# Neighbourhood attention in blocks of 16 rows by 8 columns, with q, k and v ordered by grid column

## The chip, the cores and the metric

The kernel runs on one core of a Trainium2 chip. The metric is device time in microseconds of one execution, as the median of several runs; smaller is better. One execution is also profiled, and all views quoted here are of such a profile.

## What is computed

One mixer layer over 1024 tokens of width 1024, in float32. The tokens form a grid of 16 rows by 64 columns (row = t // 64, column = t % 64).

```
h = x @ W_in                          # q, k, v, z of two groups of 8 heads of 64
group A: each token attends to a window of 8 rows x 16 columns of the grid,
         clamped inside it, with a learned bias per head and relative position
group B: each token attends to |i - j| <= 128, rotary q and k, 2 k/v heads, a sink logit
y = concat(A * silu(z_a), B * silu(z_b)) @ W_out
x = LayerNorm(2**0.25 * x + y) * gain + bias
```

The window of group A is `r0 = clip(r - 4, 0, 8)` to `r0 + 8` in rows and `c0 = clip(c - 8, 0, 48)` to `c0 + 16` in columns.

## The kernel before

Every matmul with float32 data is made of 16-bit halves (high and low part): three matmuls for one product. The projections are 21 groups of 128 columns of W_in in the order of the list `ORDER`; 24 matmuls of 512 tokens make one half of a group in a PSUM bank `ps_pj` (line 379). q and k of a head pair are evicted by `split_q` and `split_k`: ScalarE writes the high part (L257), VectorE the low part (L263), and for k GpSimd copies both to the other 64 partitions (`dup_`, L295). Each works on one half of the tokens and one head, a tile of 64 partitions by 512.

Attention goes in 128 units of 128 queries, first the 64 of group B, then the 64 of group A. A unit passes through stages, one step of a loop apart, and each step of the loop issues by hand, for different units, in this order:

- `stage_load` (seven steps ahead): the bias of group A from DRAM (SP queue) and its scaling on GpSimd (L788)
- `stage_qk`: two matmuls (L816, L817) into one of four PSUM banks `ps_s`, then VectorE adds the bias and takes the row's extreme (L826)
- `stage_exp`: the exponential on ScalarE (L842)
- `stage_tr`: the probabilities' high part on ScalarE (L852) and low part on VectorE (L853), and a DMA transpose of both (SP queue)
- `stage_pv`, for four units at once: three matmuls of 64 columns for each chunk of keys (L881); `stage_on` divides by the sum (L890)
- `stage_ot`: four transposes on TensorE (L901), then the product with the gate z on VectorE (L904 for group B, L910 for group A)

Between these, the matmuls of the later projections (`FILL`) and of the first part of the output projection are issued in proportion to the steps: item n of `FILL` starts at step `FILL_AT[n]` and ends at `FILL_AT[n + 1]`. So q0 runs from step 49 to 57, q1 from 66 to 74, q2 from 81 to 89, z2 to 97, k3 to 105, q3 to 112 and z3 to 121. The first unit of group A is at step 64, and each pair of heads (`p`) takes 16 steps. Engines execute their own instructions in the order in which they were issued. `need` issues what a unit depends on if that is still queued, and `pop` issues queued side work, a little per step.

In group A a unit is 8 rows by 16 columns of queries: four column blocks `b`, two halves of the rows. Its keys are 11 or 12 rows of 24 or 32 columns (`NROW`, `WINW`), read from the k tile as rows of a strided view; the softmax and the values take 12 rows, in three chunks of 96 or 128 keys. The q columns are put in the order of blocks by the projection's moving operand. The values are written to DRAM (`vd`, `v_part`), copied there into four column windows (`vwin`, `window`), and loaded from these for each head pair and block (`va`, `gather_v`). The bias is loaded in three pieces for each head.

The tiles `va` (values, and the rotary's scratch) are six buffers of 2 KB a partition, the tiles `bs` (bias) five.

Of the kernel before, what the change touches and what calls it, by code (L numbers as in the profile page):

```python
# [40 lines left out]
WIN_AT = [186, 202, 218, 234]  # L41
VA_AT = [46, 49, 52, 55]
VA_STEP = [(0, 1, 1), (0, 1, 3), (1, 0, 1), (1, 0, 3)]
# [8 lines left out]
WIN0 = (0, 8, 24, 40)  # L52
WINW = (24, 32, 32, 24)
NROW = (11, 12)
NKEY = tuple(12 * w for w in WINW)
BOFF = (0, 23 * WINW[0], 23 * WINW[0], 23 * (WINW[0] + WINW[1]))
BTOT = 23 * (WINW[0] + WINW[1] + WINW[3])
# [4 lines left out]
def hybrid_block(ctx, tc, xT, x, wt, wv, wo, bias, sink, gain, lbias, cos, sin, bmask, out):  # L62
# [15 lines left out]
    vd = dram.tile([4, S, 256], F16, name="vd")  # L78
    vwin = [dram.tile([4, ROWS, WINW[b] * 256], F16, name=f"vwin{b}") for b in range(4)]
# [188 lines left out]

    def split_q(p, half, src, dep=None):
        sl = slice(512 * half, 512 * half + 512)  # L270
# [12 lines left out]
    def split_k(p, half, src, dep=None):  # L283
        sl = slice(512 * half, 512 * half + 512)
# [3 lines left out]
        for j in range(2):  # L288
            a, o = slice(64 * j, 64 * j + 64), slice(64 - 64 * j, 128 - 64 * j)
            hi, lo = split_hl(lambda j=j, a=a: own("kh", p, j)[a, sl], lambda j=j, a=a: own("kl", p, j)[a, sl],  # L290
                              src[a], dep is None, eng)

            def dup_(w, j=j, a=a, o=o):
                t = own(w, p, j)
                nc.gpsimd.tensor_copy(t[o, sl], t[a, sl])  # L295
# [9 lines left out]
    def rope(ps, half):  # L305
# [3 lines left out]
        raw = tiles["ap"].tile([128, 512], F32, tag="va", name="rp_raw", bufs=6)  # L309
        sw = tiles["ap"].tile([128, 512], F32, tag="va", name="rp_sw", bufs=6)  # L310
# [94 lines left out]
    with ExitStack() as vctx:  # L405
# [276 lines left out]
        def v_part(t):  # L682
            if t > 0:
# [52 lines left out]
    def gather_v(p, b):  # L736
        w = WINW[b]
        t = ap.tile([128, 4, 256], F16, tag="va", name=f"va{p}_{b}", bufs=6)
        bulk["last"] = bulk["step"]
        nc.sync.dma_start(t[:4 * w], vwin[b][p].rearrange("(g i) (c e) -> (i c) g e", g=4, e=256))  # L740
        va[p, b] = t

    def unit_list():
        us = []
        for p in range(4):
            for j in range(2):
                for i in range(8):
                    us.append(("b", p, j, i, i % 2 == 1))
        for p in range(4):
            for j in range(2):  # L750
                for b in range(4):
                    for half in range(2):
                        us.append(("a", p, j, (b, half), half == 1))
        return us
# [11 lines left out]
    def geom(u):  # L766
        g, p, j, t, _ = u
        if g == "a":
            b, half = t
            w = WINW[b]  # L770
            return NKEY[b], [4 * w] * 3
        lo, hi = max(t - 1, 0), min(t + 2, 8)
        return 128 * (hi - lo), [128] * (hi - lo)

    def stage_load(u, i):
        g, p, j, t, _ = u
        n, _c = geom(u)
        if g == "a":
            b, half = t
            if half == 0 and b != 2:  # L780
                bulk["last"] = clock["step"] + 1
                bt = ap.tile([128, 23 * WINW[1]], F32, tag="bs", name="bias", bufs=BR)
                o, m = BOFF[b], 23 * WINW[b]
                nc.sync.dma_start(bt[:, :m], bias[2 * p + j, :, o:o + m])
                bv = bt[:, :m]
                ld = Op("sp", None, [], 1)
                ld.step = i
                op = enq("pool", lambda: nc.gpsimd.tensor_scalar(bv, bv, rsg, -1.0, op0=ALU.mult, op1=ALU.mult),  # L788
                         ld, prio=0)
                st["bias"] = bt, op  # L790
            o = 11 * WINW[b] * half
            st[u, "b"] = st["bias"][0][:, o:o + NROW[half] * WINW[b]], st["bias"][1]

    def stage_qk(u):
        g, p, j, t, _ = u
        n, _c = geom(u)
        ps = bank("s")
        m, end = n, 384
        if g == "a":
            b, half = t  # L800
# [4 lines left out]
            bias_t, op = st.pop((u, "b"))  # L805
            need(op)
            init = 3e38
        else:
            q = stks["q", f"b{p}", j][:, 128 * t:128 * t + 128]
            lo = max(t - 1, 0) * 128  # L810
# [5 lines left out]
        nc.tensor.matmul(ps[:, :m], q, sl[0], start=True, stop=False)  # L816
        nc.tensor.matmul(ps[:, :m], q, sl[1], start=False, stop=True)  # L817
        s0 = sns[units.index(u) % 2]
        sn = s0[:, end - m:]
        if g == "b" and t < 2:  # L820
            nc.vector.tensor_copy(s0[:, 384:385], nsk[:, h:h + 1])
        elif units.index(u) == 64:
            nc.vector.memset(s0[:, 384 - WINW[1]:384], -NEG)
        nm = ap.tile([128, 1], F32, tag="nm", name="nm", bufs=6)
        c = min(p, 1) if g == "b" else 2
        nc.vector.tensor_tensor_reduce(sn[:, :m], ps[:, :m], bias_t, sg[:, c:c + 1], init,  # L826
# [18 lines left out]
    def stage_tr(u):  # L845
        g, p, j, t, _ = u
        n, ch = geom(u)
        pt = st.pop((u, "p"))
        c, m = ch[0], len(ch)
        hl = split[units.index(u) % NSPLIT]  # L850
        src = pt[:, :n].rearrange("p (k c) -> p k c", c=c)
        nc.scalar.activation(hl[:, :m, 0, :c], src, AF.Copy, scale=PSCALE)  # L852
        nc.vector.scalar_tensor_tensor(hl[:, :m, 1, :c], src, PSCALE, hl[:, :m, 0, :c],  # L853
# [5 lines left out]
    def quad(q):  # L859
        g, p, j, t, _ = units[4 * q]  # L860
        return g, p, j, t // 4 if g == "b" else t[0] // 2

    def stage_pv(q):
        ps = st[q, "o"] = bank("t")
        for m in range(4):
            u = units[4 * q + m]
            g, p, j, t, _ = u
            n, ch = geom(u)
            tr = st.pop((u, "tr"))
            c = ch[0]  # L870
            mms = []
            for i in range(len(ch)):
                if g == "a":
                    b, half = t
                    v = [va[p, b][:c, i + half, 128 * j + 64 * e:128 * j + 64 * e + 64] for e in range(2)]
                else:
                    v = [vb[:, max(t - 1, 0) + i, p // 2, e, :] for e in range(2)]
                ph, pl = tr[:c, 2 * i, :], tr[:c, 2 * i + 1, :]
# [14 lines left out]
    def stage_ot(q):  # L893
# [11 lines left out]
        else:  # L905
            for i in range(2):
                b = 2 * h + i
                z = zt[p].rearrange("p (r c) -> p r c", c=GW)[:, :, 16 * b:16 * b + 16]
                src = ps[:, 256 * i:256 * i + 256].rearrange("p (r c) -> p r c", c=16)
                nc.vector.scalar_tensor_tensor(z, src, z_col(p), z, op0=ALU.mult, op1=ALU.mult)  # L910

    for b in range(4):
        at(WIN_AT[b], window, b)
# [267 lines left out]
    for i in range(-LD, NU + LO):  # L1181
# [7 lines left out]
        if i in VA_AT:  # L1189
            gather_v(0, VA_AT.index(i))  # L1190
# [22 lines left out]
        if i < NU:  # L1213
            u = units[i]
            if u[3] in (0, 4):
                need(*stk_ops[f"b{u[1]}", u[2], u[3] // 4])
            if u[3] == (0, 0):
# [17 lines left out]
        if 0 <= q < NU // 4:  # L1235
            g, p, j, h = quad(q)
            if g == "a" and p < 3 and (j, h, m) in VA_STEP:
                gather_v(p + 1, VA_STEP.index((j, h, m)))
# [15 lines left out]
def _host(inputs):  # L1254
# [22 lines left out]
    bt = np.full((8, 128, BTOT), NEG, np.float32)  # L1277
    rr, cc = np.divmod(np.arange(128), 16)
    for half in range(2):
        for b in (0, 1, 3):  # L1280
            r, c = rr + 8 * half, cc + 16 * b
            kr = np.repeat(np.arange(NROW[half]) + 4 * half, WINW[b])
            kc = np.tile(np.arange(WINW[b]) + WIN0[b], NROW[half])
            r0, c0 = np.clip(r - 4, 0, 8), np.clip(c - 8, 0, 48)
            ok = ((kr[None] >= r0[:, None]) & (kr[None] < r0[:, None] + 8)
                  & (kc[None] >= c0[:, None]) & (kc[None] < c0[:, None] + 16))
            pi, ki = np.nonzero(ok)
            o = BOFF[b] + half * 11 * WINW[b]
            bt[:, pi, o + ki] = rpb[:, kr[ki] - r[pi] + 7, kc[ki] - c[pi] + 15]
# [35 lines left out]
```

## Time and profile before

| | before |
|---|---|
| median of 3 runs | 447.23 us (445.42 to 447.49) |
| span of the profiled execution | 444.7 us; the time of that execution itself is not listed apart |
| TensorE busy | 437.5 us, 3289 matmuls |
| VectorE, ScalarE, GpSimd busy | 344.2, 308.3, 221.6 us |
| DMA | 81.39 MB in 133841 packets |

The span runs from the first instruction to the last. L12 stands for line 12 of the kernel. PE is TensorE's matmul, PEld its weight loads, DVE VectorE, ACT ScalarE, POOL GpSimd, SP the engine that issues the DMAs. In a row of the timeline stand start and duration in us, the engine, the line, the operation and its tiles; in a row of a group the count, the total busy us, the mean ns of one, and the idle time of the engine just before them with what ended it. In a row of waits stand who waited for whom, and then the total us, the number of waits and the longest.

### The profile page before, as it was taken

The page shows a single profiled execution, that of the slowest core. Times are in us where ns is not written, and L with a number is a line of the kernel's source. Part 1 is how long each engine was busy: PE and PEld are TensorE (multiplying, and loading weights), DVE is VectorE, ACT ScalarE, POOL GpSimd, SP SyncE. Part 2 cuts the span into 40 slices and gives each one's busy share as a digit, 9 for nine tenths or more (in the row PEclk, how much of TensorE's full clock was granted, in tenths as well). Part 3 has the DMA queues.
Part 4 walks back from the last instruction along what each step waited for, and adds up shares of the span by engine and source line. Part 5 has one row for each costly group of instructions (what it writes and reads, how often), then busy time and mean ns, then how long its engine had stood idle before and what let it go on. Part 6 is the DMA issues. An engine that isn't in the chain of part 4 may idle for free.

```text
span 444.7 us, 9505 instructions
## 1 busy us (share of the span) xinstructions
PE 437.5 (98%) x3289; PEld 255.5 (57%) x3289; DVE 344.2 (77%) x849; ACT 308.3 (69%) x700; POOL 221.6 (50%) x235
## 2 busy tenths in 40 slices
PE   9999999999999999999999999999999999999994
PEld 8997754444445565655565655656555654444453
DVE  5978967438986898887988888888878837589944
ACT  5759789766499988887868887888778946302401
POOL 0110074646839558866506767765574405205740
PEclk9999999999999999999999999999999999999997
DMA  8921469984659999587978899998999998103612
GB/s 272 390 91 60 145 235 339 336 292 169 213 127 214 206 190 181 98 162 143 164 127 175 169 182 180 213 170 213 192 204 253 167 172 347 55 0 102 232 69 72
DMA packets 133841, 81.39 MB, mean 183 GB/s; under 512 B 101280, under 2 KB 113440, under 8 KB 133536
## 3 DMA queue, kind: packets, MB, share of 16 engines
q1 hardware_dynamic: 133648, 80.64, 75.4%
q8 instruction: 26, 0.43, 0.4%
q14 instruction: 23, 0.19, 0.2%
q10 hardware_dynamic: 144, 0.13, 0.1%
HBM read 50.34 MB, written 9.96 MB: 136 GB/s over the span
## 4 chain that ended last, share of the span: by engine, by line
PE 91%; DMA 3%; POOL 3%; DVE 1%; issue 1%; ACT 1%; SPq 0%; POOLq 0%; DVEq 0%; ACTq 0%
PE ps_pj L379 44%; PE ps_s L1031 9%; PE ps_s L486 6%; PE ps_t L881 6%; PE ps_pj L1031 5%; PE ps_t L1031 5%; PE ps_s L816 4%; PE ps_s L817 4%; PE ps_pj L486 3%; PE ps_t L486 3%; DMA bias<-in_bias 3%; PE ps_t L901 1%; POOL wl L205 1%; PE ps_t L412 1%; POOL ks L295 1%
## 5 line engine op out<-in xcount | busy, mean ns | idle before, releaser
L379 PE MATMUL ps_pj<-xf,wh 128*128 128x512 f16 x672 | 202.1, 379 | 0.1
L379 PE MATMUL ps_pj<-xf,wl 128*128 128x512 f16 x336 | 127.3, 379 | 0.0
L379 PEld LDWEIGHTS <-wh 128*128 128x128 f16 x672 | 63.7, 98 | 60.4 <-DVE ks L263 0.5
L842 ACT ACTIVATE ps_s<-sn,nm 128x385 f32<-128x385 f32 (+3 forms) x128 | 70.1, 548 | 25.1 <-DVE nm L826 24.6
L853 DVE SCALAR_TENSOR_TENSOR split<-ps_s,split 128x384 f16<-128x384 f32 (+2 forms) x128 | 65.7, 513 | 27.5 <-ACT split L852 25.9
L1031 PEld LDWEIGHTS <-m 128*128 128x128 f16 x432 | 40.0, 98 | 41.1 <-DVE m L939 0.2
L852 ACT ACTIVATE split<-ps_s 128x384 f16<-128x384 f32 (+2 forms) x128 | 57.8, 452 | 2.5 <-DMA tr<-split 0.2
L204 POOL TENSOR_SCALAR wr<-wr,wsc 128x512 f32<-128x512 f32 x26 | 20.6, 791 | 68.1 <-ACT wh L199 61.6
L379 PEld LDWEIGHTS <-wl 128*128 128x128 f16 x336 | 32.9, 98 | 37.4
L826 DVE CUSTOM_DVE_ANT_0 sn<-ps_s,bm,nsk 128x384 f32<-128x384 f32 (+1 forms) x64 | 40.7, 636 | 2.0 <-PE ps_s L817 1.7
L1031 PE MATMUL ps_s<-wo,m 128*128 128x512 f16 (+1 forms) x192 | 40.8, 366 | 0.0
L816 PE MATMUL ps_s<-ks,qs 128*128 128x384 f16 (+4 forms) x128 | 39.2, 306 | 0.3 <-DVE qs L263 0.3
L817 PE MATMUL ps_s<-ks,qs 128*128 128x384 f16 (+4 forms) x128 | 39.2, 306 | 0.0
L826 DVE CUSTOM_DVE_ANT_0 sn<-ps_s,bias,sg 128x264 f32<-128x264 f32 (+1 forms) x64 | 35.0, 547 | 4.5 <-issue 1.5
L881 PEld LDWEIGHTS <-tr 128*128 128x128 f16 (+1 forms) x1104 | 36.6, 98 | 2.2
L205 POOL TENSOR_TENSOR wl<-wr,wh 128x512 f16<-128x512 f32 x26 | 32.7, 1257 | 2.2
L788 POOL TENSOR_SCALAR bias<-bias,rsg 128x552 f32<-128x552 f32 (+1 forms) x24 | 19.1, 797 | 23.8 <-DMA bias<-in_bias 22.6
L295 POOL COPY ks<-ks 64x512 f16<-64x512 f16 x40 | 26.0, 661 | 7.1 <-DVE ks L263 2.8
L1086 ACT ACTIVATE sd<-mv,eps 128x1 f32<-128x1 f32 x8 | 2.4, 295 | 36.5 <-DVE mv L1084 35.2
L1031 PE MATMUL ps_pj<-wo,m 128*128 128x512 f16 (+1 forms) x144 | 26.2, 326 | 0.0
L1130 POOL TENSOR_TENSOR xr<-xr,gb 128x512 f32<-128x512 f32 x7 | 9.8, 1396 | 32.4 <-ACT xr L1127 32.4
L842 ACT ACTIVATION_READ_ACCUMULATOR ps_s<-sn,nm 128x1 f32 x128 | 24.4, 190 | 0.0
(188 smaller groups left out, 813.8 us busy)
## 6 DMA issues: line engine op xcount, KB each, us to landing
ws<-in_wt SPq DMA_DIRECT2D x15, 512.0 KB, 5.9
wr<-in_wt SPq DMA_DIRECT2D x26, 256.0 KB, 3.6
wor<-in_wo SPq DMA_DIRECT2D x22, 256.0 KB, 3.5
bias<-in_bias SPq DMA_DIRECT2D x16, 276.0 KB, 3.3
xr<-in_x SPq DMA_DIRECT2D x8, 512.0 KB, 9.6
out<-xr SPq DMA_DIRECT2D x15, 256.0 KB, 2.1
bias<-in_bias SPq DMA_DIRECT2D x8, 368.0 KB, 3.8
wvraw<-in_wv SPq DMA_DIRECT2D x9, 320.0 KB, 5.8
```

The costliest lines, as they stand in the source:

```text
L205: nc.gpsimd.tensor_sub(l, raw, h)
L295: nc.gpsimd.tensor_copy(t[o, sl], t[a, sl])
L379: nc.tensor.matmul(ps, a[:, k % 4, :], mv, start=(k == 0 and i == 0), stop=(k == KT - 1 and i == 2))
L486: nc.tensor.matmul(ps[:, :320], lh[:, ts], rh[:, cs], start=(k == ko[0] and i == 0), stop=(k == ko[-1] and i == 2))
L816: nc.tensor.matmul(ps[:, :m], q, sl[0], start=True, stop=False)
L817: nc.tensor.matmul(ps[:, :m], q, sl[1], start=False, stop=True)
L826: nc.vector.tensor_tensor_reduce(sn[:, :m], ps[:, :m], bias_t, sg[:, c:c + 1], init, op0=ALU.add, op1=ALU.min, accum_out=nm)
L842: nc.scalar.activation(pt[:, :m], sn[:, :m], AF.Exp, bias=nm, scale=-1.0, accum_out=sm[:, k:k + 1])
L852: nc.scalar.activation(hl[:, :m, 0, :c], src, AF.Copy, scale=PSCALE)
L853: nc.vector.scalar_tensor_tensor(hl[:, :m, 1, :c], src, PSCALE, hl[:, :m, 0, :c], op0=ALU.mult, op1=ALU.subtract)
L881: nc.tensor.matmul(ps[:, HD * m:HD * m + HD], a, b_, start=(i == 0), stop=(i == len(mms) - 1))
L1031: nc.tensor.matmul(ps, lh[:, ts], rh[:, cs], start=(e == EO[0] and i == 0), stop=(e == EO[-1] and i == 2))
```

## The change

A unit of group A is now 16 rows by 8 columns: eight blocks `t` of 128 queries. q, k and v of group A are stored by grid column (column major, 16 rows to a column), so a block and its two neighbours are a contiguous band of three blocks of 128 keys, two at either edge. The units of both groups have the same shape now, and `geom` serves both.

- `split_q` and `split_k` read the PSUM bank with a step of 64 elements (`taken_from`) and write eight neighbouring rows of each column (`place`); the copies of `dup_` have the same shape, 64 x 64 x 8. Group B's are as they were, as is the projection of q, which no longer reorders.
- `v_part` stores `vd` by column, in two DMAs of 64 partitions instead of one of 128; the copies into windows are gone, and `gather_v` loads all values of a head pair at once, a tile of 128 x 8 x 256.
- The bias is one load of 128 x 896 for a head (edge, inner and edge block), and one scaling.
- `va` and the bias share one set of six buffers of 4 KB a partition.
- The product with z takes 512 elements at once, walking z with a step of 64 elements.

```diff
+    def place(t, a, half, by_col):
+        if not by_col:
+            return t[a, 512 * half:512 * half + 512]
+        return t[a].rearrange("p (c r) -> p c r", r=ROWS)[:, :, 8 * half:8 * half + 8]
+
+    def taken_from(src, a, by_col):
+        return src[a].rearrange("p (r c) -> p c r", c=GW) if by_col else src[a]
...
-            hi, lo = split_hl(lambda j=j, a=a: own("q", p, j)[a, sl], lambda j=j, o=o: own("q", p, j)[o, sl],
-                              src[a], dep is None, eng)
+            hi, lo = split_hl(lambda j=j, a=a: place(own("q", p, j), a, half, col),
+                              lambda j=j, o=o: place(own("q", p, j), o, half, col),
+                              taken_from(src, a, col), dep is None, eng)
...
-                nc.gpsimd.tensor_copy(t[o, sl], t[a, sl])
+                nc.gpsimd.tensor_copy(place(t, o, half, col), place(t, a, half, col))
...
-                    if name[0] == "q" and name[1] != "b":
-                        mv = mv.rearrange("p (r b c) -> p b r c", b=4, r=8)
...
-                nc.sync.dma_start(
-                    vd[:, 128 * (t - 1):128 * t, :].rearrange("q p e -> p q e"),
-                    vt[:, 0:8].rearrange("p (q h) i e -> p q (h i e)", h=2))
+                for i in range(2):
+                    nc.sync.dma_start(
+                        vd[:, :, 2 * (t - 1) + i, :].rearrange("q c e -> c q e"),
+                        vt[GW * i:GW * i + GW, 0:8].rearrange("p (q h) i e -> p q (h i e)", h=2))
...
-    def window(b):
-        bulk["last"] = bulk["step"]
-        nc.sync.dma_start(vwin[b], vd.rearrange("q (r c) e -> q r (c e)", c=GW)[
-            :, :, 256 * WIN0[b]:256 * (WIN0[b] + WINW[b])])
+    def gather_v(p):
+        t = va[p] = big_ap([128, 8, 256], F16, f"va{p}")
         bulk["last"] = bulk["step"]
+        nc.sync.dma_start(t, vd[p].rearrange("(k c) r e -> (c r) k e", k=8))
...
+        if g == "a" and t == 0:
+            bulk["last"] = clock["step"] + 1
+            bt = big_ap([128, BWIN[3]], F32, "bias")
+            nc.sync.dma_start(bt, bias[2 * p + j])
...
         if g == "a":
-            b, half = t
-            m, end = NROW[half] * WINW[b], 384 if half else 384 - WINW[1]
-            q = stks["q", p, j][:, 512 * half + 128 * b:512 * half + 128 * b + 128]
-            sl = [stks[w, p, j].rearrange("p (r c) -> p r c", c=GW)[
-                :, 4 * half:4 * half + NROW[half], WIN0[b]:WIN0[b] + WINW[b]] for w in ("kh", "kl")]
+            q = stks["q", p, j][:, 128 * t:128 * t + 128]
+            sl = [stks[w, p, j][:, lo:lo + n] for w in ("kh", "kl")]
...
-            for i in range(2):
-                b = 2 * h + i
-                z = zt[p].rearrange("p (r c) -> p r c", c=GW)[:, :, 16 * b:16 * b + 16]
-                src = ps[:, 256 * i:256 * i + 256].rearrange("p (r c) -> p r c", c=16)
-                nc.vector.scalar_tensor_tensor(z, src, z_col(p), z, op0=ALU.mult, op1=ALU.mult)
+            z = zt[p].rearrange("p (r c) -> p c r", c=GW)[:, 32 * h:32 * h + 32, :]
+            nc.vector.scalar_tensor_tensor(z, ps.rearrange("p (c r) -> p c r", r=ROWS), z_col(p), z,
+                                           op0=ALU.mult, op1=ALU.mult)
...
-            if u[3] == (0, 0):
+            if u[0] == "a" and u[3] == 0:
                 need(*stk_ops[u[1], u[2], 0], *stk_ops[u[1], u[2], 1])
```

More of the change, by code (lines that the diff above doesn't have):

```diff
@@ L76, in bank @@
         return (ps1 if bufs == 1 else ps2).tile([128, 512], F32, tag=tag, name=f"ps_{tag}", bufs=bufs)
[L78 to L79 removed]
+    vd = dram.tile([4, GW, ROWS, 256], F16, name="vd")
     taken = [0]
@@ L766, in geom @@
     def geom(u):
-        g, p, j, t, _ = u
-        if g == "a":
-            b, half = t
[L770 to L800, printed above, removed]
-            m, end = NROW[half] * WINW[b], 384 if half else 384 - WINW[1]
-            q = stks["q", p, j][:, 512 * half + 128 * b:512 * half + 128 * b + 128]
-            sl = [stks[w, p, j].rearrange("p (r c) -> p r c", c=GW)[
-                :, 4 * half:4 * half + NROW[half], WIN0[b]:WIN0[b] + WINW[b]] for w in ("kh", "kl")]
-            bias_t, op = st.pop((u, "b"))
+        g, p, j, t = u
@@ new lines, in geom, with stage_load @@
+        lo, hi = max(t - 1, 0), min(t + 2, 8)
+        return 128 * (hi - lo), hi - lo
+    def stage_load(u, i):
+        g, p, j, t = u
+        if g == "a" and t == 0:
+            bulk["last"] = clock["step"] + 1
+            bt = big_ap([128, BWIN[3]], F32, "bias")
+            nc.sync.dma_start(bt, bias[2 * p + j])
+            ld = Op("sp", None, [], 1)
+            ld.step = i
+            op = enq("pool", lambda: nc.gpsimd.tensor_scalar(bt, bt, rsg, -1.0, op0=ALU.mult, op1=ALU.mult),
+                     ld, prio=0)
+            st["bias", p, j] = bt, op
@@ L806, in stage_qk @@
+    def stage_qk(u):
+        g, p, j, t = u
+        n, _m = geom(u)
+        ps = bank("s")
+        lo = max(t - 1, 0) * 128
+        if g == "a":
+            q = stks["q", p, j][:, 128 * t:128 * t + 128]
+            sl = [stks[w, p, j][:, lo:lo + n] for w in ("kh", "kl")]
+            b = (t > 0) + (t == 7)
+            bias_t, op = st["bias", p, j]
             need(op)
+            bias_t = bias_t[:, BWIN[b]:BWIN[b + 1]]
             init = 3e38
@@ L859, in quad @@
     def quad(q):
-        g, p, j, t, _ = units[4 * q]
-        return g, p, j, t // 4 if g == "b" else t[0] // 2
+        g, p, j, t = units[4 * q]
+        return g, p, j, t // 4
     def stage_pv(q):
```

118 lines of the change are left out of this document (48 added, 70 removed).

## The prediction, made before the result was known

> **What bounds the kernel now.** I read the page first, then the busy time by stretches, then who kept TensorE waiting, then the chain of waits for TensorE's own rates.
>
> ```profile
> span 444.7 us, 9505 instructions
> PE 437.5 (98%) x3289; PEld 255.5 (57%) x3289; DVE 344.2 (77%) x849; ACT 308.3 (69%) x700; POOL 221.6 (50%) x235
> ```
>
> TensorE is busy 437.5 us of a span of 444.7. Busy matmuls overlap in this profile, so 98% alone doesn't show that none was late. The stretches and the waits do:
>
> ```profile
> 220.00:293.00 73.00, 72.90 (x647) 41.91 (x645) 61.35 (x169) 57.55 (x149) 42.08 (x54) 1.00 0.91 175
> 293.00:333.00 40.00, 39.74 (x375) 23.02 (x373) 32.63 (x91) 32.35 (x83) 27.90 (x34) 1.00 1.05 195
> ...
> sum 235.00, PE 234.64 PEld 134.66 DVE 196.38 ACT 193.92 POOL 147.49; mean PE 58.66 PEld 33.67 DVE 49.10 ACT 48.48 POOL 36.87
> ```
>
> ```profile
> PE ps_s L816 <- DVE qs L263: 0.3, 1, 0.3
> ```
>
> ```profile
> PEld L816 <- DVE qs L263: 0.7, 1, 0.7
> PEld L379 <- DVE ks L263: 0.5, 1, 0.5
> ```
>
> These are two of four stretches and the sum of all four, 121 to 356 us; the columns are length, TensorE, weight loads, VectorE, ScalarE, GpSimd (instructions in brackets), then TensorE's granted clock, DMA share and GB/s. From 121 us (the first attention unit) to 356 (the last) TensorE is busy 234.64 of 235. The three rows beneath, from the two lists of what TensorE and its weight loads waited for, are all that attention cost it: 0.3, 0.7 and 0.5 us. Every other wait in attention, DMA's included, is covered. So less work on another engine shortens nothing: the time moves with TensorE's work, or with a wait that becomes long enough to reach TensorE.
>
> The span is 444.7 us; the three runs are 445.42 to 447.49 with median 447.23, so 2.5 us lie around the span. I make the sum on the span and carry it to the median: 447.2 plus what is added.
>
> **TensorE's own work.** The chain of waits has uninterrupted pieces (start, length, what):
>
> ```profile
> 68.72 10.38 PE ps_pj L379 x48
> ...
> 286.33 1.05 PE ps_t L881 x36
> ```
>
> 48 matmuls of 512 columns take 10.38 us: 0.422 ns a column, overhead included. 36 probability-by-value matmuls take 1.05 us: 29 ns each. Before, a head's eight neighbourhood units have 264, 288, 352 and 384 keys, twice each: 2576 columns a pass. After, six have 384 and two have 256: 2816. That is 240 more x 2 passes (kh, kl) x 8 heads = 3840 columns, or +1.6 us. The value side had three chunks in all 64 units and now has two in the 16 edge units: 16 x 3 = 48 matmuls fewer, -1.4 us. Net **+0.2 us**. Nothing else leaves TensorE; the 16-element pieces in which it read x for q go, but every 512-column matmul holds the same rate.
>
> **A head that starts on fresh q.** In row order unit 112 (head pair 3) reads only the first half of q3; the second half is read by unit 113. In column order every block of 128 queries takes 8 rows from each half, so unit 112 needs both. Only pair 3 is tight: `FILL_AT` ends q3 at step 112, its first unit is step 112; q0, q1, q2 end at 57, 74, 89 for steps 64, 80, 96. The timeline around it:
>
> ```profile
> 330.32 0.38 PE L379 MATMUL ps_pj<-xf,wl 128*128 128x512 f16 x1
> ...
> 330.54 0.28 PE L816 MATMUL ps_s<-ks,qs 128*128 128x264 f16 x1
> ...
> 330.91 0.58 ACT L257 ACTIVATE qs<-ps_pj 64x512 f16<-64x512 f32 x1
> ...
> 331.41 0.59 PE L379 MATMUL ps_pj<-xf,wh 128*128 128x512 f16 x2
> 331.52 0.68 DVE L263 SCALAR_TENSOR_TENSOR qs<-ps_pj,qs 64x512 f16<-64x512 f32 x1 [0.81 <-ACT qs L257]
> ...
> 332.26 0.10 PEld L816 LDWEIGHTS <-qs 128*128 128x128 f16 x1 [0.75 <-DVE qs L263]
> 332.26 0.30 PE L816 MATMUL ps_s<-ks,qs 128*128 128x288 f16 x1 [0.26 <-DVE qs L263]
> ```
>
> The 264-column L816 is unit 112, right behind the last q3 matmul. ScalarE then takes the high part of the second half (L257), VectorE the low part (L263), and unit 113 (288 columns) starts at 332.26. In the changed program the last q3 matmul is still the one in front of unit 112, and unit 112 now waits for that low part. TensorE's queue is in order, so z3's matmuls behind it wait too: 332.26 - 330.54 = 1.72 us idle. The wait of unit 113 goes: two matmuls from 331.41 at 0.216 end their slots at 331.84, so 0.42 us. Net **+1.3 us**, with passes as long as today's.
>
> **Wider units on VectorE and ScalarE.**
>
> ```profile
> L853 DVE SCALAR_TENSOR_TENSOR split<-ps_s,split 128x384 f16<-128x384 f32 x80 | 44.4, 555 | 18.4 <-ACT split L852 17.2 <-POOL wl L205 0.4
> L826 DVE CUSTOM_DVE_ANT_0 sn<-ps_s,bias,sg 128x384 f32<-128x384 f32 x16 | 9.8, 610 | 0.3 <-PE ps_s L817 0.2
> L826 DVE CUSTOM_DVE_ANT_0 sn<-ps_s,bias,sg 128x352 f32<-128x352 f32 x16 | 9.2, 578 | 1.2 <-issue 0.9 <-PE ps_s L817 0.2
> L826 DVE CUSTOM_DVE_ANT_0 sn<-ps_s,bias,sg 128x288 f32<-128x288 f32 x16 | 8.2, 511 | 0.3
> L826 DVE CUSTOM_DVE_ANT_0 sn<-ps_s,bias,sg 128x264 f32<-128x264 f32 x16 | 7.8, 489 | 2.7 <-POOL wl L205 0.8 <-issue 0.6 <-POOL ws L204 0.6
> L853 DVE SCALAR_TENSOR_TENSOR split<-ps_s,split 128x288 f16<-128x288 f32 x32 | 14.6, 455 | 6.5 <-ACT split L852 6.3
> L853 DVE SCALAR_TENSOR_TENSOR split<-ps_s,split 128x256 f16<-128x256 f32 x16 | 6.7, 422 | 2.6 <-ACT split L852 2.4
> ```
>
> A head's bias passes (L826) take 2 x (610 + 578 + 511 + 489) = 4.38 us; after, 6 x 610 + 2 x 481 (264 columns less 8 at 1 ns) = 4.62. Its low-part passes (L853) go from 4 x 455 + 4 x 555 = 4.04 to 6 x 555 + 2 x 422 = 4.17. Together +0.38 us a head, 3 us in 115 us; ScalarE's exp and copy grow by the same elements. This lies beside TensorE; its cover is VectorE's idle time, next.
>
> **Column-ordered passes.** The evictions of q and k (4 pairs x 2 halves x 2 heads x q and k = 32 on ScalarE, L257, and 32 on VectorE, L263) now walk PSUM at 64 elements a step, eight of each column, and the gate product (L910) walks z the same way.
>
> ```profile
> L263 DVE SCALAR_TENSOR_TENSOR qs<-ps_pj,qs 64x512 f16<-64x512 f32 x16 | 11.0, 688 | 1.2 <-ACT qs L257 0.8
> L257 ACT ACTIVATE qs<-ps_pj 64x512 f16<-64x512 f32 x16 | 9.4, 586 | 4.9 <-DVE qs L263 4.9
> L910 DVE SCALAR_TENSOR_TENSOR z<-ps_t,zc,z 128x256 f32<-128x256 f32 x16 | 7.0, 477 | 7.8 <-PE ps_t L901 7.8
> L904 DVE SCALAR_TENSOR_TENSOR z<-ps_t,zc,z 128x512 f32<-128x512 f32 x8 | 6.0, 747 | 0.0
> ```
>
> 256 elements in pieces of 16 neighbours take 477 ns and 512 in one piece 747: 1.05 ns an element, jumps between pieces free. A single-element step stands in no row. Bounds for the extra of a pass: below, nothing (a gain is excluded: same elements, already one at a time); above, its elements paid once more, 512 x 1.05 = 0.54 us. The nearest row still takes 16 neighbours at each stop and shows only that the jump is free, not that a new place for every element is. I take **0.40**, nearer the upper end, and keep both ends. At unit 112 one such ScalarE pass and one VectorE pass stand in line: **+0.8 us** (0 to 1.1). Elsewhere they eat idle time of VectorE:
>
> ```profile
> 221.00:293.00 72.00, 13.58 (x20) 1.00 0.91 176
> ```
>
> ```profile
> DVE split L853 <- ACT split L852: 10.0, 18, 0.8
> ```
>
> Of the stretch 220 to 293, VectorE works 61.35 of 73 us; 20 of these passes lie in it, and 10.0 us of its idle time are waits for ScalarE's copy. Adding 20 x 0.40 = 8.0, 3.5 heads x 0.38 = 1.3, and 0.4 for two gate products (each one strided pass of 0.75 + 0.40 for two of 0.48) makes 71.0. 2.0 us of slack remain where 10.0 us were waits, which shorten as VectorE falls behind but don't vanish, because the ScalarE passes grow too (57.55 + 8). What doesn't fit reaches TensorE through the four `s` banks: the scores of a unit need the bank that the low part four units earlier frees. I take **+2.0 us**, an estimate (0 to 5). In 293 to 333, 8 x 0.40 fits into 40 - 32.63.
>
> **GpSimd and the DMA queue, costed at nothing.**
>
> ```profile
> L295 POOL COPY ks<-ks 64x512 f16<-64x512 f16 x40 | 26.0, 661 | 7.1 <-DVE ks L263 2.8 <-ACT ks L257 1.5 <-DMA wr<-in_wt 0.6
> L788 POOL TENSOR_SCALAR bias<-bias,rsg 128x552 f32<-128x552 f32 x16 | 12.1, 755 | 18.4 <-DMA bias<-in_bias 17.5 <-DVE split L853 0.7
> L788 POOL TENSOR_SCALAR bias<-bias,rsg 128x736 f32<-128x736 f32 x8 | 7.1, 882 | 5.4 <-DMA bias<-in_bias 5.1
> ```
>
> ```profile
> 324.55 0.73 POOL L788 TENSOR_SCALAR bias<-bias,rsg 128x552 f32<-128x552 f32 x1
> ...
> 327.25 1.16 POOL L295 COPY ks<-ks 64x512 f16<-64x512 f16 x2
> ...
> 332.24 0.49 DVE L826 CUSTOM_DVE_ANT_0 sn<-ps_s,bias,sg 128x264 f32<-128x264 f32 x1
> ```
>
> 24 bias scalings (12.1 + 7.1 us) become 8 of 896 columns, about 1.0 us each by the two rows, so 11 us of GpSimd go. The one for unit 112 ends at 325.28 and is read at 332.24: 7 us cover the larger load. The 40 duplicate copies stay, 32 of them column-ordered; the last of k3 ends at 328.41, 3.85 us before the 332.26 at which q lets unit 112 go. SP loses the four window copies, 12 value loads and 16 bias loads and gains 8 stores; none was in a TensorE wait, so this gains nothing. `va` and bias now share six buffers, but each reuse lies after its reader's step (the bias of the fifth head, step 89, takes the buffer of va0, whose last values are multiplied at step 85), so no load holds up the transposes behind it.
>
> **Sum:** 447.2 + 0.2 + 1.3 + 0.8 + 2.0 = **451.5 us**.
>
> **Rivals.** (1) *Single-element steps cost nothing.* The pieces of L910 speak for it. Then 0.2 + 1.3: **448.7 us**, no change that counts. It decides below about 0.2 us a pass, where VectorE's 11.65 idle us take 4.0 + 1.5 easily. Chance 0.36.
>
> (2) *Every element is paid twice and VectorE becomes the bound.* Each pass costs 0.54: 61.35 + 20 x 0.54 + 1.3 + 0.7 = 74.2 us of work in 73; with half of the 10.0 us of waits left, some 5 us reach TensorE. 0.2 + 1.3 + 1.1 + 5 = 7.6: **454.8 us**. Against it: no row shows such a price. Chance 0.22. [...]
>
> (3) *GpSimd's column-ordered copies become the bound at unit 112.* At twice 0.61 us, the eight of k3 add 4.9 less 2.2 for bias passes gone, and 3.85 covers it. At three times, 9.8 - 2.2 - 3.85 = 3.7 us come out, from a factor of 2.4 on: 0.2 + 1.3 + 3.7, **452.4 us**. Chance 0.05.
>
> (4) *Faster: the 48 dropped value matmuls are worth their weight loads.* If each saved a whole weight load of 0.10 us (the first row at 332.26), it would be -4.8 instead of -1.4: 447.2 - 4.8 + 1.6 + 1.3 = **445.3 us**. It decides from about 90 ns a matmul on; against it stands 36 in 1.05 us, loads included. Chance 0.05.
>
> **How the numbers follow.** A change of 0.5%, 2.2 us, is about what a measurement of this kernel can tell from none; slower means above 449.4. My forecast has 0.32 and gives 450 to 453.5 by itself. Slower: 0.32 + 0.22 + 0.05 + 0.02 of rival 1's upper tail = 0.61. Same: the other 0.34 of rival 1. Faster: 0.05. The range runs from 447.8 (rival 1 with half of its wait at unit 112) to 456.5 (rival 2 with 7 us through the banks); about 0.15 lies outside.
>
> **What would show it.** In the profile after: 528 `va` matmuls at 29 ns; unit 112's scores idle for some 1.7 us or more on the low part of q3; L263's and L257's successors at 1.0 to 1.1 us instead of 0.69 and 0.59 (0.6 to 0.7 would be rival 1, 1.15 and more rival 2); the column-ordered gate product above 1.1; TensorE waits between 220 and 293 us of about 2. The prediction is wrong if TensorE stays as dense as now around unit 112, or if a wait for a bias or value load shows on it.

## The result and the profile after

The changed kernel takes 450.58 us (median of 6 runs, 448.97 to 451.30) where the kernel before takes 447.17 (6 runs): ratio 1.0082, 95% interval 1.0060 to 1.0104. Six more runs beside the first experiments gave 451.59 us, ratio 1.0106 (1.0082 to 1.0130). The forecast was 451.5. The size came out; its terms, as the profile shows, mostly did not, so that the hit is in good part luck.

From the page of the profiled execution after (448.97 us, span 447.2), the rows that answer to those of before:

```profile
span 447.2 us, 9320 instructions
PE 437.1 (98%) x3241; PEld 252.9 (57%) x3241; DVE 349.0 (78%) x840; ACT 309.9 (69%) x700; POOL 212.0 (47%) x219
```

TensorE is busy 0.4 us less in a span 2.5 us longer: nearly all of the added time is waiting, not work. The same stretches as before (length, TensorE, weight loads, VectorE, ScalarE, GpSimd, clock, DMA share, GB/s), then what TensorE waited for:

```profile
220.00:293.00 73.00, 72.61 (x628) 41.12 (x627) 61.75 (x163) 56.90 (x147) 36.29 (x44) 1.00 0.73 131
293.00:333.00 40.00, 37.91 (x335) 21.24 (x332) 33.33 (x87) 32.45 (x83) 25.17 (x29) 1.00 0.74 147
```

```profile
PE ps_s L797 <- DVE qs L256: 2.9, 1, 2.9
...
PE ps_pj L380 <- DVE ks L256: 0.4, 1, 0.4
PE ps_s L1002 <- DVE m L910: 0.2, 1, 0.2
```

VectorE's work from 220 to 293 us went from 61.35 to 61.75, not to 71, so the column-ordered passes hardly weigh. One wait of 2.9 us carries the loss: unit 112's scores (L797) on the low part of q3 (L256). The groups by line and form say which passes became longer (count, then busy, mean ns):

```profile
L256 DVE SCALAR_TENSOR_TENSOR qs<-ps_pj,qs 64x512 f16<-64x512 f32 x16 | 11.0, 688 | 1.1 <-ACT qs L250 0.7
L250 ACT ACTIVATE qs<-ps_pj 64x512 f16<-64x512 f32 x16 | 9.4, 585 | 5.5 <-DVE qs L256 5.5
L298 POOL COPY ks<-ks 64x512 f16<-64x512 f16 x40 | 26.1, 661 | 10.3 <-DVE ks L256 3.4 <-ACT ks L250 3.0 <-PE ps_s L798 1.3
L882 DVE SCALAR_TENSOR_TENSOR z<-ps_t,zc,z 128x512 f32<-128x512 f32 x8 | 9.3, 1168 | 7.4 <-PE ps_t L876 7.4
L879 DVE SCALAR_TENSOR_TENSOR z<-ps_t,zc,z 128x512 f32<-128x512 f32 x8 | 6.0, 747 | 0.0
L773 POOL TENSOR_SCALAR bias<-bias,rsg 128x896 f32<-128x896 f32 x8 | 8.5, 1066 | 8.8 <-DMA bias<-in_bias 8.6
```

Column-ordered evictions take 688 and 585 ns, before 688 and 586; GpSimd's copies 661 as before. Only the gate product, which walks z in SBUF at a new 256-byte step for each element, grew: 1168 ns (L882) against 747 (L879). Now the timeline in front of unit 112:

```profile
330.53 0.38 PE L380 MATMUL ps_pj<-xf,wl 128*128 128x512 f16 x1
330.74 0.69 DVE L256 SCALAR_TENSOR_TENSOR qs<-ps_pj,qs 64x512 f16<-64x512 f32 x1
331.47 0.48 DVE L805 CUSTOM_DVE_ANT_0 sn<-ps_s,bias,sg 128x256 f32<-128x256 f32 x1
...
331.99 0.48 ACT L821 ACTIVATE ps_s<-sn,nm 128x256 f32<-128x256 f32 x1 [1.28 <-DVE nm L805]
...
332.50 0.57 ACT L250 ACTIVATE qs<-ps_pj 64x512 f16<-64x512 f32 x1
...
333.11 0.68 DVE L256 SCALAR_TENSOR_TENSOR qs<-ps_pj,qs 64x512 f16<-64x512 f32 x1 [0.68 <-ACT qs L250]
...
333.85 0.28 PE L797 MATMUL ps_s<-ks,qs 128*128 128x256 f16 x1 [2.94 <-DVE qs L256]
```

The last q3 matmul ends its slot at 330.75 and unit 112 starts at 333.85: 3.10 us idle, where I had 1.72. The high part (L250) starts at 332.50, 1.59 us after the matmul's record ends (330.53 + 0.38); before the change it was 0.21 us (330.70 to 330.91, the rows of the prediction). On ScalarE's queue it stands behind the exp of unit 111 (L821), which waits for that unit's minimum, which VectorE forms at 331.47, after a low part of q3's first half. From that low part (330.74) to the end of the last one (333.79) it is one chain of 3.05 us across VectorE and ScalarE. In the kernel before the same low part stood at 329.09, 1.45 us ahead of the end of the last q3 matmul's slot (330.54 in the prediction):

```profile
329.09 0.69 DVE L263 SCALAR_TENSOR_TENSOR qs<-ps_pj,qs 64x512 f16<-64x512 f32 x1
```

### The profile page after: what moved, and what is told of

It reads as the page before. It is cut to its first block, busy times and chain, and to the rows that moved or that the text cites. A ratio compares the mean times of both kernels' runs of the same rounds, so it can differ in the third digit from the quotient of the medians.

```text
span 447.2 us, 9320 instructions
## 1 busy us (share of the span) xinstructions
PE 437.1 (98%) x3241; PEld 252.9 (57%) x3241; DVE 349.0 (78%) x840; ACT 309.9 (69%) x700; POOL 212.0 (47%) x219
## 4 chain that ended last, share of the span: by engine, by line
PE 77%; DVE 10%; ACT 7%; issue 5%; DVEq 0%; ACTq 0%
PE ps_pj L380 36%; PE ps_s L1002 8%; PE ps_s L487 6%; PE ps_pj L1002 5%; PE ps_t L856 5%; PE ps_pj L487 3%; PE ps_t L487 3%; PE ps_t L1002 3%; PE ps_s L797 3%; PE ps_s L798 3%; ACT split L829 3%; ACT ps_s L821 2%; DVE split L830 2%; DVE qs L256 2%; DVE ks L256 1%
## 5 line engine op out<-in xcount | busy, mean ns | idle before, releaser
L830 DVE SCALAR_TENSOR_TENSOR split<-ps_s,split 128x384 f16<-128x384 f32 (+1 forms) x128 | 66.9, 522 | 28.9 <-ACT split L829 27.5
L821 ACT ACTIVATE ps_s<-sn,nm 128x385 f32<-128x385 f32 (+3 forms) x128 | 71.0, 554 | 26.3 <-DVE nm L805 25.6
L829 ACT ACTIVATE split<-ps_s 128x384 f16<-128x384 f32 (+1 forms) x128 | 58.6, 458 | 2.4
L797 PE MATMUL ps_s<-ks,qs 128*128 128x384 f16 (+1 forms) x128 | 40.0, 313 | 2.9 <-DVE qs L256 2.9
L798 PE MATMUL ps_s<-ks,qs 128*128 128x384 f16 (+1 forms) x128 | 40.0, 313 | 0.0
L805 DVE CUSTOM_DVE_ANT_0 sn<-ps_s,bias,sg 128x384 f32<-128x384 f32 (+1 forms) x64 | 37.0, 578 | 2.6 <-PE ps_s L798 2.0
L856 PEld LDWEIGHTS <-tr 128*128 128x128 f16 x1056 | 35.2, 98 | 2.5
L197 POOL TENSOR_SCALAR ws<-ws,wsc 128x512 f32<-128x512 f32 x16 | 11.1, 691 | 33.9 <-ACT wh L192 30.1
L821 ACT ACTIVATION_READ_ACCUMULATOR ps_s<-sn,nm 128x1 f32 x128 | 24.4, 191 | 0.0
L797 PEld LDWEIGHTS <-qs 128*128 128x128 f16 x128 | 12.5, 98 | 18.4 <-DVE qs L256 3.4
```

The source lines that it names most:

```text
L197: nc.gpsimd.tensor_scalar(raw, raw, scale, 1.0, op0=ALU.mult, op1=ALU.mult)
L797: nc.tensor.matmul(ps[:, :n], q, sl[0], start=True, stop=False)
L798: nc.tensor.matmul(ps[:, :n], q, sl[1], start=False, stop=True)
L805: nc.vector.tensor_tensor_reduce(sn[:, :n], ps[:, :n], bias_t, sg[:, c:c + 1], init, op0=ALU.add, op1=ALU.min, accum_out=nm)
L821: nc.scalar.activation(pt[:, :m], sn[:, :m], AF.Exp, bias=nm, scale=-1.0, accum_out=sm[:, k:k + 1])
L829: nc.scalar.activation(hl[:, :m, 0, :], src, AF.Copy, scale=PSCALE)
```

## The experiments

Theory 1: the added time is the wait of unit 112 for q3's second half. Rivals: (2) the column-ordered passes overload VectorE; (3) the wider units make it late; (4) loads of bias and value. A second question came with the first runs: why the time of the changed kernel spreads over 4 us.

**The changed kernel again.**

> The changed kernel again, on the chip of the three runs beside it. Every theory: 450.6 us within 0.7, 3.4 us above the kernel before.

451.59 us (449.62 to 452.87), 0.3 above the range expected, beside 446.40 for the kernel before. Its profile shows a second price that the first profile of the changed kernel did not have. Stretches around unit 112, columns as above:

```profile
330.00:334.00 4.00, 1.05 (x7) 0.42 (x6) 2.89 (x8) 2.20 (x7) 1.17 (x2) 1.00 0.46 97
334.00:335.00 1.00, 1.00 (x6) 0.42 (x5) 0.76 (x3) 0.50 (x2) 0.00 (x0) 0.96 1.14 339
335.00:338.00 3.00, 3.00 (x38) 2.31 (x37) 1.81 (x5) 2.93 (x8) 1.96 (x2) 0.50 1.32 206
338.00:340.00 2.00, 2.00 (x11) 0.89 (x10) 0.48 (x1) 0.01 (x1) 0.32 (x1) 0.91 0.84 256
```

TensorE stands idle for 3.1 us, resumes at 333.70, and from 335 to 338 us its granted clock is 0.50: about 3.4 us at half speed with the edges (0.04 + 3 x 0.50 + 2 x 0.09 = 1.7 us of full-speed time lost). Of the changed kernel's 12 runs, 8 have a mean clock of 0.987 to 0.994 and take 450.6 to 452.9 us; four have 0.997 or 0.998 and take 449.0 to 450.2. The mean clock says little by itself: the profiles of the kernel before and of the first one after the change both show a clock of 0.50 in their last microseconds (from 440 us on and from 445 us on), and runs of the kernel before have 0.994 to 1.000; it is the time together with the clock that divides the 12. Here the clock falls 1.2 us after TensorE resumes (0.96 over 334 to 335 us, so at about 334.9); what makes it fall in some runs only is not shown.

**Unread matmuls in the idle stretch.**

```diff
+        if units.index(u) == 112:
+            for _ in range(14):
+                nc.tensor.matmul(ps[:, n:512], sl[0][:, :128], sl[0][:, :512 - n], start=True, stop=True)
         nc.tensor.matmul(ps[:, :n], q, sl[0], start=True, stop=False)
```

> The changed kernel with 14 matmuls of 256 columns that nobody reads, right behind the last q3 matmul and in front of unit 112's scores; they write the unused half of the scores' bank and read only k3, which is long there. They fill about 1.5 us of the 3.1 us in which TensorE stood idle, and unit 112 starts no earlier. Theory 1b (the idle 3.1 us costs twice: its own length, and in most runs some 3.4 us at half the granted clock behind it): the idle stretch becomes 1.6 us, no stretch at 0.50 follows, every run is near the fastest ones of the changed kernel, median 449.4, 1 to 2 us under it. Theory 1a (only the length of the wait counts, and the clock falls for other reasons): no change, 451.0. If the added matmuls delay something: above 451.

449.43 us, all six runs within 449.18 and 449.77, mean clock 0.996 to 0.998. What TensorE waited for, and the timeline:

```profile
PE ps_s L800 <- DVE qs L256: 1.4, 1, 1.4
```

```profile
331.28 1.69 PE L799 MATMUL ps_s<-ks 128*128 128x256 f16 x14
334.41 0.28 PE L800 MATMUL ps_s<-ks,qs 128*128 128x256 f16 x1 [1.44 <-DVE qs L256]
```

Work that nobody reads lowers the ratio from 1.0106 to 1.0059 (1.0038 to 1.0081), 2 us, and takes the spread away: unit 112 starts no earlier (3.1 us after the last q3 matmul, 331.28 to 334.41), but the clock stays at 1.00 in each microsecond from 329 to 339. 449.43 is also the time of the four runs above at 0.997 or 0.998 (449.4 on average). So the wait had two prices.

**Six unread matmuls instead of 14.**

> As the run with 14 unread matmuls in front of unit 112, but with 6 (0.65 us), so that TensorE stands idle for some 2.45 us. It tells where between 1.7 us (no fall of the clock seen) and 3.1 us (a stretch at half the clock in most runs) the second price starts. If the fall needs an idle stretch near 3 us: all runs near 449.4, as with 14. If it grows with the idle stretch: some runs of the four at 450.5 or above, fewer than with 3.1 us.

450.18 us (four runs): 449.55 and 449.78 at mean clock 0.998, 450.58 and 451.07 at 0.995 and 0.994. TensorE's wait in the profiled run is 2.3 us, and no half-clock stretch follows it there (1.00 in each microsecond from 332 to 339). The other two runs look like runs with one; four are too few for a share, and I don't call it shown.

**q3 three units earlier.** In `FILL_AT`, k3's entry (the third number here) and q3's (the fourth) move.

```diff
-... 89, 97, 105, 112, 121, ...
+... 89, 97, 103, 109, 121, ...
```

> The changed kernel with the projection of q3 ending at step 109, three units ahead of unit 112, and not right in front of it. Theory 1 (the added time is the wait of unit 112 for the second half of q3): unit 112's scores wait for nothing, the 3.1 us idle of TensorE at 331 us go, and the time falls by 2.5 to 3.1 us against the changed kernel, to about 447.8; what is left over the kernel before is within 1 us. Theory 2 (the column-ordered passes overload VectorE and ScalarE) and theory 3 (the 384-wide units do): the late work is the same, so the wait moves to another unit and the time falls by less than 1 us. Theory 4 (bias and value loads): no change.

448.04 us, ratio 1.0037 (1.0020 to 1.0055), 3.5 us under the changed kernel beside it; neither wait nor half clock is left at unit 112 (TensorE busy and its clock 1.00 in each microsecond from 329 to 341). Theory 1 holds against 2 and 4: the two prices together are what went. But 1.6 us (0.9 to 2.5) stay over the kernel before, where I had expected 1 at most. Some is given back: z3's matmuls are spread thinner, and the output projection waits at 352 us for the bank that z3 frees:

```profile
PE ps_pj L1002 <- DVE z L345: 1.1, 1, 1.1
```

**The same shift in the kernel before.**

> The kernel before with the projection of q3 ending at step 109: the control to the second run. Theory 1: only the 0.4 us in front of unit 113 are there to be won, 446.8. If the earlier end of q3 is worth something of its own (less crowded VectorE at the end of attention), it shows here as more than 1 us.

450.38 us, ratio 1.0080 (1.0060 to 1.0100): my 446.8 was wrong by 3.6 us. The waits of TensorE, and two stretches:

```profile
PE ps_t L881 <- DMA tr<-split: 2.7, 2, 1.8
```

```profile
345.00:350.00 5.00, 2.86 (x40) 2.08 (x38) 4.03 (x14) 4.93 (x14) 1.50 (x2) 1.00 1.10 299
350.00:355.00 5.00, 4.46 (x22) 2.04 (x23) 2.71 (x8) 2.59 (x7) 3.93 (x5) 0.66 1.06 213
```

Two groups of value products catch up with the transposed tiles they read; that fewer z3 matmuls between them let it happen is argued, not tested. TensorE idles 2.7 us between 347 and 350.5 with nine matmuls in the middle, and then runs at 0.66 of its clock from 350 to 355, a loss of (1 - 0.66) x 5 = 1.7 us. The second price again, in a kernel without any part of the change.

**Half of the mechanism alone, in the kernel before.** Its units keep row order, width and loads; each column block's second half is taken first, so unit 112 reads the half of q3 that is evicted last (the bias load, the columns of sums and values and `need` follow the new order).

```diff
-                    for half in range(2):
-                        us.append(("a", p, j, (b, half), half == 1))
+                    for half in (1, 0):
+                        us.append(("a", p, j, (b, half), half == 0))
```

> The kernel before, row-ordered and with its old units, but each column block's two units taken second half first, so that unit 112 reads the half of q3 that is evicted last. Nothing else of the change is in it. Theory 1: TensorE idles 1.7 us or more in front of unit 112, against 0.4 in front of unit 113 before, and the time rises by 1.3 to 2.7 us over the kernel before, to 448.5 to 449.9. Theories 2 to 4: no column-ordered pass, no wider unit and no other load is in it, so the time stays within 0.5 us of the kernel before.

447.92 us, ratio 1.0025 (1.0010 to 1.0040): 0.4 to 1.8 us more than the kernel before, 1.1 at the middle, where 1.3 was the least that I had expected; the wait itself decides. What TensorE waited for, then VectorE's and TensorE's timelines:

```profile
PE ps_s L816 <- DVE qs L263: 1.6, 1, 1.6
```

```profile
329.24 0.69 DVE L263 SCALAR_TENSOR_TENSOR qs<-ps_pj,qs 64x512 f16<-64x512 f32 x1
329.96 0.49 DVE L826 CUSTOM_DVE_ANT_0 sn<-ps_s,bias,sg 128x264 f32<-128x264 f32 x1
...
331.64 0.68 DVE L263 SCALAR_TENSOR_TENSOR qs<-ps_pj,qs 64x512 f16<-64x512 f32 x1 [0.81 <-ACT qs L257]
```

```profile
330.42 0.38 PE L379 MATMUL ps_pj<-xf,wl 128*128 128x512 f16 x1
332.38 0.30 PE L816 MATMUL ps_s<-ks,qs 128*128 128x288 f16 x1 [1.58 <-DVE qs L263]
```

The last matmul's slot ends at 330.64, so TensorE idles 1.74 us: the 1.72 of the prediction, and no fall of the clock (1.00 in each microsecond from 329 to 341). The chain is as long as after the change (329.24 to 332.32, 3.08 us; after, 3.05). What differs is its start: 1.40 us ahead of the end of the last matmul here, at that end after the change. VectorE comes 1.4 us late.

**Why VectorE is late.**

```diff
+        w = 256 if 105 <= units.index(u) <= 110 else n
-        nc.vector.tensor_tensor_reduce(sn[:, :n], ps[:, :n], bias_t, sg[:, c:c + 1], init,
+        nc.vector.tensor_tensor_reduce(sn[:, :w], ps[:, :w], bias_t[:, :w], sg[:, c:c + 1], init,
```

(and so for exp, high and low part of these units.)

> The changed kernel with VectorE's and ScalarE's four passes (bias, exp, high and low part) of the six units 105 to 110, in front of unit 112, over 256 of their 384 columns; all matmuls stay. The third key block of these units is left out of their softmax. VectorE loses 6 x (0.132 + 0.134) = 1.6 us of work there, ScalarE 6 x 0.2 = 1.2. The open point: the chain to unit 112 was forecast at 1.72 us, measured 1.74 in the kernel before with its halves swapped, and 3.1 in the changed kernel, where VectorE came to it some 1.4 us later. If the width of the passes makes it late (theory 3 for this place): the idle stretch falls to 2.3 us or less, and with it the half clock, median 448.5 to 449.7. If something else does (the order of the passes on VectorE): it stays at 2.8 to 3.1 us, and the time at 450 to 451.6.

448.30 us (eight runs), ratio 1.0039 (1.0026 to 1.0052). The timelines of VectorE and TensorE:

```profile
330.30 0.69 DVE L256 SCALAR_TENSOR_TENSOR qs<-ps_pj,qs 64x512 f16<-64x512 f32 x1
...
332.67 0.68 DVE L256 SCALAR_TENSOR_TENSOR qs<-ps_pj,qs 64x512 f16<-64x512 f32 x1 [0.81 <-ACT qs L250]
```

```profile
331.42 0.38 PE L380 MATMUL ps_pj<-xf,wl 128*128 128x512 f16 x1
333.41 0.28 PE L797 MATMUL ps_s<-ks,qs 128*128 128x256 f16 x1 [1.61 <-DVE qs L256]
```

With 256-column passes in the six units ahead, the chain starts 1.34 us before the last matmul's slot ends (331.64) and the idle time is 1.77 us, as in the kernel before with swapped halves; the time went lower than the 448.5 that I had put as the least. So how much VectorE and ScalarE have to do ahead of unit 112 sets the wait: 1.3 us of it went, and by the mean clocks the slow stretch too (0.995 to 1.000 in these eight runs, 0.987 to 0.994 in the changed kernel's slower eight). How much of that is the change's own width this run does not tell. It takes 1.6 us of VectorE's work away, where the change had put in some 0.5 in these six units (472 elements in the bias and low-part passes, the rows of the prediction at about 1.04 ns each). And the traces show VectorE late before they begin. Scores and low part of unit 104, before and after the change:

```profile
314.15 0.28 PE L816 MATMUL ps_s<-ks,qs 128*128 128x264 f16 x1
317.35 0.45 DVE L853 SCALAR_TENSOR_TENSOR split<-ps_s,split 128x288 f16<-128x288 f32 x1
```

```profile
314.34 0.27 PE L797 MATMUL ps_s<-ks,qs 128*128 128x256 f16 x1
318.90 0.43 DVE L830 SCALAR_TENSOR_TENSOR split<-ps_s,split 128x256 f16<-128x256 f32 x1
```

The low part comes 3.20 us after the scores before and 4.56 after: 1.36 of the 1.4 us are there at unit 104. They build up over the forty units ahead: 0.2 us at unit 72, 0.6 at unit 80, 0.8 at unit 97.

**q3 earlier by 1.5 units, and 368 keys.** The first run sets `104, 110.5` for `103, 109`, the second adds the 368 keys (bias slice, high and low part and value products follow), the third is the kernel before with the first's shift, the fourth has 368 keys and q3 2 units earlier (`103.6, 110`).

```diff
-        return 128 * (hi - lo), hi - lo
+        return 128 * (hi - lo) - (16 if g == "a" and 0 < t < 7 else 0), hi - lo
```

> The changed kernel with q3 ending 1.5 units ahead of unit 112 (not 3), so that z3's matmuls stay denser in the last units of attention. Theory 1: 1.5 units of 2.3 us cover the 3.1 us wait; unit 112 waits for nothing or under 0.5 us, and the 1.3 us that TensorE lost at 351 us with the 3-unit shift shrinks: 447.0 to 447.9. Theories 2 and 3 (VectorE and ScalarE carry too much): what stays over the kernel before, 1.5 us or more, is not moved by where q3 lies: 448.0 or above.

> The run before with the six inner units of each neighbourhood head at 368 keys, not 384: the last grid column of the third block lies in no query's window. 1536 columns of scores fewer at 0.422 ns are 0.65 us of TensorE; each of the 96 bias, exp, copy and low-part passes loses 16 elements, about 0.017 us. Theory 1: 0.65 us under the run before, 446.4 to 447.3, level with the kernel before. Theory 3 (the 384-wide units make VectorE and ScalarE late): more than 1 us under it.

> The kernel before with the same 1.5-unit shift of q3, the control to the two runs above. Theory 1: the 0.42 us in front of unit 113 go, nothing else: 446.0 to 446.5. The 3-unit shift cost the kernel before 4 us by value matmuls that waited for a transposed tile at 347 us with the value and output-weight loads on the same queue; if a thinner stream of z3 matmuls lays that bare already at 1.5 units: 447.5 or above, with idle of TensorE at 345 to 352 us.

> 368 keys, and q3 ending 2 units ahead of unit 112 (not 1.5). With 1.5 units TensorE still stood 1.1 us idle there. Theory 1: half a unit more is 1.1 us, so that idle time goes and the time is 0.5 to 1.1 us below the run with 1.5 units, 445.9 to 446.5, level with the kernel before or 0.5 under it. If z3's thinner stream costs as much behind unit 112 as it did at 3 units (1.3 us at 351 us), it stays at 446.9 or above.

| kernel | median us | ratio to before | 95% interval |
|---|---|---|---|
| changed, q3 1.5 units earlier | 447.44 | 1.0015 | 1.0000 to 1.0029 |
| the same with 368 keys | 446.95 | 1.0007 | 0.9992 to 1.0022 |
| before, q3 1.5 units earlier | 447.18 | 1.0009 | 0.9994 to 1.0025 |
| changed, 368 keys, q3 2 units earlier | 447.93 | 1.0024 | 1.0009 to 1.0039 |

The times of the first two came as expected: the ratio falls from 1.0106 to 1.0015 with two numbers in a table, though 1.1 us of idle time stay at unit 112; 16 keys less are worth 0.5 us at the median, about TensorE's columns alone, and no more than the intervals can tell from nothing. They do show in VectorE's lag: the low part of unit 97 comes 4.69 us after its scores, 5.02 in the first run, 4.19 in the kernel before. With 16 keys less, 192 of the 368 elements a head that the change added to the bias and low-part passes are gone, and 0.33 of the 0.83 us. If the other 176 count alike, the width makes some 0.6 of it, an estimate; the longer gate product (1.17 us for two of 0.48) is the other work added to VectorE, and its share was not tested alone. The fourth missed: about half of that idle time went (0.5 us of wait is left), but the wait for z3's bank at 351 us came back (1.1 us). The third missed too: it gained nothing, and 1.0 us of waits for transposed tiles, as in the 3-unit shift, stand in its profile. No version beats the kernel before; the second is level with it.

**The gate product in four forms.**

```diff
+            zin, zout = ((z, z), (z, sc), (sc, z), (flat, flat))[p]
```

> The changed kernel with the gate product (512 columns) in four forms, one to a head pair: pair 0 reads and writes z by grid column, as in the change; pair 1 reads by column and writes a contiguous scratch tile (z is then cleared); pair 2 reads the scratch tile and writes z by column; pair 3 reads and writes contiguously. So the gate of pairs 1 to 3 is not computed as the reference has it. Known: both by column 1168 ns, contiguous in the other group's heads 747 ns. If a new place for each read costs: pair 1 about 1.17, pair 2 about 0.75 us. If for each write: the other way round. If each costs half: both 0.95 us. Pair 3: 0.75.

The group of this line by its tiles (min/median/max ns):

```profile
L888 DVE SCALAR_TENSOR_TENSOR z<-ps_t,zc,z x4: 751/954/1161, 281.3 to 375.0; 128x512 f32<-128x512 f32 x4
L888 DVE SCALAR_TENSOR_TENSOR scr<-ps_t,zc,z x2: 1086/1095/1104, 310.2 to 318.5; 128x512 f32<-128x512 f32 x2
L888 DVE SCALAR_TENSOR_TENSOR z<-ps_t,zc,scr x2: 1118/1126/1133, 345.8 to 353.0; 128x512 f32<-128x512 f32 x2
```

The first row holds pairs 0 and 3 together: contiguous 751 at the least, both by column 1161 at the most. Reading by column alone takes 1095, writing alone 1126: each costs nearly the whole of the 0.4 us, and together they cost little more. None of the three outcomes that I had listed. This profile (451.5 us, the one run) has the half clock behind unit 112 too, after a wait of 3.0 us:

```profile
336.00:339.00 3.00, 3.00 (x38) 2.18 (x36) 2.11 (x7) 2.86 (x8) 1.66 (x2) 0.50 1.44 215
```

## Why the prediction came out

**TensorE's own work, +0.2: right.** Summed from start to next start over the records, waits taken off, the scores take 1.6 us more and the value products 1.3 us less: +0.3. Beside it stands a wait that no term has, for an eviction of k right behind a group of value products; what made it was not tested. It is TensorE's one wait between 220 and 293 us, where 2 us were forecast:

```profile
271.81 0.61 PE L380 MATMUL ps_pj<-xf,wh 128*128 128x512 f16 x2 [0.39 <-DVE ks L256]
```

**A head that starts on fresh q, +1.3: the right place and mechanism, a term too small.** 1.72 us is what it takes with the passes of the kernel before (1.74 with its halves swapped). The step that failed is "with passes as long as today's": it read the chain from the last matmul on, ScalarE free at 330.91, and did not look at what stands ahead on ScalarE's and VectorE's queues if VectorE is later. Measured 3.10 - 0.42 = 2.7 us.

**Wider units, costed beside TensorE: wrong at this one place.** The passes are as long as worked out (611 and 479 ns in the bias pass), and elsewhere VectorE's idle time takes them. But that idle time does not bring VectorE back: its lag grew over group A to the 1.4 us by which it came late at unit 112, where a matmul waits for an eviction and nothing covers it. By the runs with 368 keys the wider units make most of that lag; their exact share, beside the gate product's, stays open.

**Column-ordered passes, +0.8 and +2.0: nothing in the evictions.** I took 0.40 us a pass from rows that couldn't show it; the evictions measure 0.00. Rival 1 had that right, and its 448.7 fails by the wait and the clock. Rival 2 falls with it: no run shows its 0.54 us a pass. The evictions, which read one float32 per 256 bytes of PSUM, stay at 688 and 585 ns; only the eight gate products, which walk z in SBUF, come near its price, 0.42 us each (1168 ns against 747).

**The clock: not in the prediction at all.** Each stretch that I had quoted showed 1.00. Two thirds of the runs pay about 2 us for it: the mean of the eight is 451.5, of the other four 449.4.

**GpSimd, DMA, bias and value loads at nothing: right.** GpSimd went from 221.6 to 212.0 us, the bias scalings to 1066 ns each, and none of these is in a wait of TensorE. Rivals 3 and 4 did not occur: the copies stayed at 661 ns, and the 48 value matmuls were worth 1.3 us, not 4.8.

So 451.5 was met by luck: an excess of 2.8 us for passes that cost nothing stood against a lack of 1.4 us of wait at unit 112, 0.5 elsewhere and, in most runs, 2 us of clock. The cause, q3 arriving right in front of its first reader, stands: with two thirds of that wait gone the change costs 0.7 us (0.0 to 1.3).

## What to carry to other kernels

Here a step behind a just-produced operand started where its engine's queue let it, not at the producer's end (L250, 1.59 us after the last q3 matmul): before costing a new wait, list what is queued ahead of each link on its engine, and shift that by the work the change adds. A wait of TensorE near 3 us should, by these runs, be priced twice, once for its length (3.1 us) and once for the clock (1.7 us of full-speed time in the profile that shows the fall); filling it, even with work nobody reads, can pay (2 us here). Before giving up a layout, look at the hand-set order around it: two entries of one table held most of this change's loss.

## What was not expected of the hardware

- Single-element steps of 256 bytes through PSUM cost ScalarE and VectorE nothing in these evictions (585 and 688 ns for 512 elements, with 16-byte pieces on the SBUF side), while float32 elements at 256-byte steps in SBUF add 0.35 us to a read of 512, 0.38 to a write, 0.42 to both.
- In three profiles the clock stood at 0.50 in attention: for about 3.4 us after a wait of 2.9 us (3.1 us idle; the changed kernel again), for 3.0 us or more after one of 3.0 (the gate product in four forms), and for about 3.4 us after two idle pieces of 2.7 us in all with nine matmuls between (0.66 over five us; the kernel before with q3 three units earlier). The first profile after the change, also with a wait of 2.9 us, has no such stretch (1.00 in each microsecond from 329 to 341), nor have the one with 2.3 us of wait and the kernel before with swapped halves, 1.74 us idle. The length of one wait does not decide alone: at the end of the kernel before, the clock falls to 0.50 at about 439.8 us, 0.6 us after a wait of 1.8 us:

```profile
439.23 0.67 PE L1111 MATMUL ps_t<-xr,dr 128*128 128x256 f32 x2 [1.81 <-ACT dr L1109]
```

```profile
439.30:440.00 0.70, 0.70 (x3) 0.62 (x4) 0.70 (x3) 0.07 (x1) 0.00 (x0) 0.88 0.00 0
440.00:442.00 2.00, 0.69 (x2) 0.00 (x0) 0.56 (x1) 0.37 (x1) 0.00 (x0) 0.50 0.23 71
```
